# A row softmax on one core: tiles of twelve rows in four buffers, each divided and stored before the next tile's maximum

## Chip, cores and metric

The kernel runs on one core of a Trainium2 chip. The metric is the device time in microseconds, lower is better. DVE is VectorE, ACT is ScalarE, POOL is GpSimd and SP is SyncE; SBUF is the on-chip memory, in 128 partitions. A semaphore is a counter by which one engine, or a transfer, tells another that it is done.

## The reference

```python
batch, seq, dim = 32, 512, 1024          # x: float32, temperature 0.5

def reference(x, temperature):
    scaled = x / temperature
    shifted = scaled - np.max(scaled, axis=-1, keepdims=True)
    exp_x = np.exp(shifted)
    return (exp_x / np.sum(exp_x, axis=-1, keepdims=True)).astype(np.float32)
```

There are 16384 rows of 1024 numbers: 67.1 MB are read and 67.1 MB written.

## The kernel before

A tile gives each of the 128 SBUF partitions eight consecutive rows, so one partition's share is a piece of 32 KiB, contiguous in memory. Loads are issued from SP, stores from ACT. Every load after the first six has to wait for the store that frees its buffer, and six buffers take 192 KiB of each partition. The arithmetic goes in groups of four rows: one maximum on DVE (and a small multiplication that makes the exponentials' bias of it), four exponentials with their sums on ACT, one reciprocal and four multiplications ("divide") on DVE.

```python
TILES = [[8]] * 16
BUFS = 6
GROUP = 4
# ... pools, and `groups`: (tile, first row, rows, the part to store after it)

    def load():
        i = len(tiles)
        if i < len(TILES):
            xt = data.tile([P, sum(TILES[i]), d], f32, name="xt")
            nc.sync.dma_start(out=xt, in_=dram(xf, i))
            tiles.append(xt)
# ... maximum(g), exponential(g), divide(g): as described
    def store(g):
        i, _, _, part = groups[g]
        if part:
            a, k = part
            nc.scalar.dma_start(out=dram(of, i)[:, a : a + k, :], in_=tiles[i][:, a : a + k, :])
            if a + k == sum(TILES[i]):
                load()

    with tc.manual_schedule():
        for _ in range(BUFS):
            load()
        for g in range(len(groups) + 1):
            if g < len(groups):
                maximum(g)
                exponential(g)
            if g > 0:
                divide(g - 1)
                store(g - 1)
```

The order is a software pipeline: group g-1 is divided after the maximum of group g, so that ACT has time for its exponentials. At a tile's end this makes the finished tile wait for the load, and then for the maximum, of the next tile.

Of the kernel before, what the change touches and what calls it, by code (L numbers as in the profile page):

```python
# [1 line left out]

# [4 lines left out]



TILES = [[8]] * 16  # L10
BUFS = 6

GROUP = 4


@with_exitstack
def kernel(
    ctx: ExitStack,
    tc: tile.TileContext,
    x: bass.AP,  # L20
    temperature: bass.AP,
    out: bass.AP,
):
    nc = tc.nc
    f32 = mybir.dt.float32
    scale = 1.0 / float(temperature)
    extreme = mybir.AluOpType.max if scale > 0 else mybir.AluOpType.min

    P = 128
    xf = x.flatten_outer_dims()  # L30
    of = out.flatten_outer_dims()
    n, d = xf.shape
    assert sum(sum(ks) for ks in TILES) * P == n

    data = ctx.enter_context(tc.tile_pool(name="data", bufs=BUFS))
    stats = ctx.enter_context(tc.tile_pool(name="stats", bufs=4))


    groups, first, r = [], [], 0
    for i, ks in enumerate(TILES):  # L40
        first.append(r)
        r += sum(ks)
        a = 0
        for k in ks:
            for b in range(0, k, GROUP):
                m = min(GROUP, k - b)
                groups.append((i, a + b, m, (a, k) if b + m == k else None))
            a += k

    def dram(t, i):  # L50
        k = sum(TILES[i])
        block = t[P * first[i] : P * (first[i] + k), :]
        return block.rearrange("(p k) d -> p k d", p=P, k=k)

    tiles, small = [], []
# [8 lines that stand above are left out]
    def maximum(g):  # L64
        i, a, k, _ = groups[g]
        top, bias, sums, recip = (
            stats.tile([P, k], f32, name=name) for name in ("top", "bias", "sums", "recip")
        )
        small.append((bias, sums, recip))
        nc.vector.tensor_reduce(  # L70
            out=top, in_=tiles[i][:, a : a + k, :], axis=mybir.AxisListType.X, op=extreme
        )
        nc.vector.tensor_scalar_mul(bias, in0=top, scalar1=-scale)  # L73

    def exponential(g):
        i, a, k, _ = groups[g]
        bias, sums, _ = small[g]
        for b in range(k):
            nc.scalar.activation(  # L79
                tiles[i][:, a + b, :],  # L80
                tiles[i][:, a + b, :],
                mybir.ActivationFunctionType.Exp,
                bias=bias[:, b : b + 1],
                scale=scale,
                accum_out=sums[:, b : b + 1],
            )

    def divide(g):
        i, a, k, _ = groups[g]
        _, sums, recip = small[g]  # L90
        nc.vector.reciprocal(recip, sums)  # L91
        for b in range(k):
            nc.vector.tensor_scalar_mul(  # L93
                tiles[i][:, a + b, :], in0=tiles[i][:, a + b, :], scalar1=recip[:, b : b + 1]
# [13 lines that stand above are left out]
        for _ in range(BUFS):  # L108
            load()
        for g in range(len(groups) + 1):  # L110
            if g < len(groups):
                maximum(g)
                exponential(g)
            if g > 0:
                divide(g - 1)
                store(g - 1)


# [1 line left out]
_INS = ['x', 'temperature']  # L120
_OUTS = [((32, 512, 1024), 'float32')]

_NUMBERS = {'temperature': 0.5}


# [26 lines left out]
```

## Time and profile before

| | before |
|---|---|
| time, median of 3 | 317.9 us (317.88 to 318.01) |
| span of the profiled execution | 316.0 us |
| DVE busy, ACT busy | 235.5 us (75%), 149.6 us (47%) |
| moved | 134.25 MB, 425 GB/s over the span |

From the page of the kernel before: the span, the DMA rows of the span cut in 40 slices (a digit is the busy share of the 16 DMA engines in tenths, 9 is 90% or more; below it is what they moved), and two groups of instructions (line, engine, operation, count, then total busy us and mean ns, then the idle time before them and its releaser).

```profile
span 316.0 us, 620 instructions
...
DMA  8999999999999999999999999999999999999996
GB/s 332 411 452 423 373 460 415 452 425 431 436 427 440 427 444 423 444 419 448 415 452 411 452 408 456 423 444 427 436 431 432 440 423 444 419 444 419 452 411 274
...
L70 DVE TENSOR_REDUCE top<-xt 128x4 f32<-128x4096 f32 x32 | 141.3, 4416 | 62.6 <-DMA xt<-in_x_dram 62.6
...
L91 DVE RECIPROCAL recip<-sums 128x4 f32<-128x4 f32 x32 | 5.5, 171 | 2.1 <-ACT xt L79 2.1
```

The DMA engines are busy in every slice but the first and the last; no compute engine is. The next lines are the view by windows: a stretch of the span in us, its length, busy time of DVE, ACT and POOL, the clock, the DMA share, and GB/s.

```profile
core 0: us, DVE busy (x) ACT busy (x) POOL busy (x), PEclk, DMA share, GB/s
2.00:34.00 32.00, 20.69 (x17) 14.63 (x24) 0.00 (x0) 1.00 0.99 422
34.00:60.00 26.00, 25.72 (x25) 14.95 (x27) 0.00 (x0) 1.00 0.99 416
60.00:120.00 60.00, 51.26 (x50) 32.29 (x57) 0.00 (x0) 1.00 1.01 436
120.00:180.00 60.00, 46.15 (x46) 29.79 (x53) 0.00 (x0) 1.00 1.00 432
180.00:240.00 60.00, 44.57 (x43) 29.19 (x51) 0.00 (x0) 1.00 1.00 434
308.00:312.00 4.00, 0.00 (x0) 0.00 (x0) 0.00 (x0) 1.00 1.04 451
312.00:316.00 4.00, 0.00 (x0) 0.00 (x0) 0.00 (x0) 1.00 0.21 90
```

The rate is 416 to 422 GB/s from 2 to 60 us and 432 to 436 from 60 to 240 us; the last transfers are over about 2 us before the end. The two DVE groups on the page show that DVE has time to spare: ahead of its maxima (L70) it is idle for 62.6 us, ended by loads, and ahead of its reciprocals (L91), where it would wait for ACT, for 2.1 us.

The stores, by the view of their source line (durations in ns of the issuing instruction, then the start of the first and of the last issue in us): the first store is issued at 32.7 us.

```profile
L101 ACTq DMA_DIRECT2D out_dram<-xt x16: 338/338/374, 32.7 to 302.4; - x16
```

### The profile page before, as it was taken

Reading aid. Unit: us, or ns where it says so; the run is one execution under the profiler, and the core shown is the slowest. Engines: PE = TensorE matmul, PEld = TensorE weight load, DVE = VectorE, ACT = ScalarE, POOL = GpSimd, SP = SyncE. Lnnn points to the kernel's source line nnn. Section 1 sums busy time; section 2 is a strip of 40 time slices with the busy share of each in tenths; the row PEclk is TensorE's granted clock in tenths of the full one; section 3 lists DMA queues with packets and bytes.
Section 4 is the critical chain, followed back from the end, with each engine's and each line's share of the span. In section 5 each row is a group of like instructions: output and inputs, shape, how many; then the busy total and the mean of one; then the engine's idle time right before and its main releaser. Section 6 shows DMA issues by size and latency. Waiting matters only on the chain.

```text
span 316.0 us, 620 instructions
## 1 busy us (share of the span) xinstructions
DVE 235.5 (75%) x224; ACT 149.6 (47%) x257; POOL 0.2 (0%) x4
## 2 busy tenths in 40 slices
DVE  0399999999689494994949859497693976949720
ACT  0176666666526255361554605546064560645500
POOL 0000000000000000000000000000000000000000
DMA  8999999999999999999999999999999999999996
GB/s 332 411 452 423 373 460 415 452 425 431 436 427 440 427 444 423 444 419 448 415 452 411 452 408 456 423 444 427 436 431 432 440 423 444 419 444 419 452 411 274
DMA packets 4612, 134.25 MB, mean 425 GB/s; under 512 B 512, under 2 KB 512, under 8 KB 512
## 3 DMA queue, kind: packets, MB, share of 16 engines
q1 hardware_dynamic: 2304, 67.11, 49.7%
q10 hardware_dynamic: 2304, 67.11, 49.2%
q14 instruction: 4, 0.03, 0.0%
HBM read 67.11 MB, written 67.11 MB: 425 GB/s over the span
## 4 chain that ended last, share of the span: by engine, by line
DVE 49%; DMA 32%; another core or an unknown queue 9%; ACT 5%; issue 1%; DVEq 0%; SPq 0%
DVE top L70 29%; DMA xt<-in_x_dram 20%; DVE xt L93 18%; DMA out_dram<-xt 12%; ACT xt L79 5%; DVE recip L91 1%; DVE bias L73 1%; DVEq L147 0%; SPq L61 0%
## 5 line engine op out<-in xcount | busy, mean ns | idle before, releaser
L79 ACT ACTIVATE xt<-xt,bias 128x1024 f32<-128x1024 f32 x128 | 145.4, 1137 | 136.8 <-DVE recip L91 119.4
L70 DVE TENSOR_REDUCE top<-xt 128x4 f32<-128x4096 f32 x32 | 141.3, 4416 | 62.6 <-DMA xt<-in_x_dram 62.6
L93 DVE TENSOR_SCALAR xt<-xt,recip 128x1024 f32<-128x1024 f32 x128 | 87.7, 749 | 1.1
L79 ACT ACTIVATION_READ_ACCUMULATOR xt<-xt,bias 128x1 f32 x128 | 23.9, 187 | 0.0
L79 ACT ACT_TABLE_LOAD x1 | 1.3, 1283 | 13.0 <-DMA xt<-in_x_dram 13.0
L91 DVE RECIPROCAL recip<-sums 128x4 f32<-128x4 f32 x32 | 5.5, 171 | 2.1 <-ACT xt L79 2.1
L73 DVE TENSOR_SCALAR bias<-top 128x4 f32<-128x4 f32 x32 | 5.4, 170 | 1.1
L133 POOL MEMSET const-bfloat16-1.0<- 128x1 bf16 x1 | 0.1, 101 | 0.0
L133 POOL MEMSET const-uint8-127<- 128x1 uint8 x1 | 0.1, 101 | 0.0
L133 POOL MEMSET const-float32-0.0<- 128x1 f32 x1 | 0.1, 98 | 0.2 <-issue 0.2
L133 POOL MEMSET const-float32-1.0<- 128x1 f32 x1 | 0.1, 98 | 0.0
## 6 DMA issues: line engine op xcount, KB each, us to landing
xt<-in_x_dram SPq DMA_DIRECT2D x16, 4096.0 KB, 50.2
out_dram<-xt ACTq DMA_DIRECT2D x16, 4096.0 KB, 38.6
```

The source lines that it names most:

```text
L70: nc.vector.tensor_reduce(out=top, in_=tiles[i][:, a : a + k, :], axis=mybir.AxisListType.X, op=extreme)
L73: nc.vector.tensor_scalar_mul(bias, in0=top, scalar1=-scale)
L79: nc.scalar.activation(tiles[i][:, a + b, :], tiles[i][:, a + b, :], mybir.ActivationFunctionType.Exp, bias=bias[:, b : b + 1], scale=scal ...
L91: nc.vector.reciprocal(recip, sums)
L93: nc.vector.tensor_scalar_mul(tiles[i][:, a + b, :], in0=tiles[i][:, a + b, :], scalar1=recip[:, b : b + 1])
L133: nc = _bacc.Bacc("TRN2", target_bir_lowering=False, num_devices=1)
```

## The change

The intent: fewer and larger transfers (22 instead of 32, pieces of 48 KiB instead of 32) in the same 192 KiB, and stores that go out earlier, since a tile's last group is divided before the next tile's maximum.

```diff
@@ -7,8 +7,8 @@
 
 
 
-TILES = [[8]] * 16
-BUFS = 6
+TILES = [[12]] * 10 + [[8]]
+BUFS = 4
 
 GROUP = 4
 
@@ -108,10 +108,14 @@
         for _ in range(BUFS):
             load()
         for g in range(len(groups) + 1):
+            same = 0 < g < len(groups) and groups[g][0] == groups[g - 1][0]
+            if g > 0 and not same:
+                divide(g - 1)
+                store(g - 1)
             if g < len(groups):
                 maximum(g)
                 exponential(g)
-            if g > 0:
+            if same:
                 divide(g - 1)
                 store(g - 1)
```

On DVE the order of instructions changes at tile ends only; the counts and shapes do not.

## The prediction

> **What bounds the kernel now.** The DMA engines. The page shows a DMA share of 9 tenths or more in every slice but the first and last, and 425 GB/s over the 316.0 us span; the busiest compute engine, DVE, has 75%. By stage (busy time per window): 422 GB/s from 2 to 34 us (loads only), 416 to 60 us, then 436, 432, 434 and 430 up to 290 us. The Trainium skill ("DMA: Bandwidth & Descriptors", Where 436 GB/s comes from) puts the fabric's ceiling at 435 GB/s; this trace agrees, its steady state stands at about 433. 134.2 MB at 433 GB/s take 310 us. The other 6 us are the first 2 us (164 GB/s, about 1.2 us lost), the weak stretch up to 60 us (about 2 us) and the last 4 us (90 GB/s, about 3.2 us, mostly the last store's completion). The chain of waits shows much DVE only because it runs back through work that transfers hide: DVE still waits 62.6 us for loads.
>
> **What the change does.** Bytes, compute instructions and their shapes stay (32 maxima of 4.42 us, 128 divisions of 0.75 us, 128 exponentials).
> - A tile's last four rows are divided before the next tile's maximum. Now DVE often waits 4.5 to 5 us for the next load, and then 4.4 us of maximum: stores go out about 9.5 us earlier. In exchange DVE waits at each tile's end for the exponential: four rows take 4.65 us, a division group (2.9 us) covers part, so about 1.8 us a tile. A tile of twelve then costs DVE about 3 x (4.42 + 0.17 + 0.2 + 2.74) + 1.8 = 24.4 us; its load and store cost the DMA 12.58 MB / 433 = 29 us. DMA stays the limit, with 5 us to spare.
> - 22 transfers instead of 32, pieces of 48 KiB instead of 32. Packet time is 98.9% of 16 engines' span over 4096 large packets, 1.22 us each, against 1.20 at 435 GB/s: at most 1.5 us in total can be won from larger pieces.
> - The same 192 KiB per partition. The first tile lands after about 17.5 us instead of 13, the first store goes out near 42 us instead of 32.7. The four first loads last 58 us, so nothing runs dry; loads only, at 422 instead of 433 GB/s, cost 0.3 us more.
> - Tail: now the last store is issued at 302.4 and lands in 12.8 us, almost alone. In a schedule worked out by hand from these durations, the new last store (eight rows) is issued some 10 us before the one ahead of it has drained, so the tail stays full: worth 0 to 1 us.
>
> **On the critical path.** Almost nothing of the 9.5 us per tile: two queues with a backlog keep the engines full whichever gets work earlier. The sum is about 1 us won.
>
> **Prediction.** 316.9 us, range 314.4 to 319.6. Faster by over 2%: 3%; within 2%: 94%; slower by over 2%: 3%.
>
> **What would show it.** Right: DMA share 9 tenths in all inner slices, 428 to 435 GB/s steady; DVE busy unchanged at 235 us; its waits for ACT rise from 2.1 to about 20 us; large packets 2816 instead of 4096; last store landing in about 20 us.
>
> **What would make it wrong.** A piece of 48 KiB that the engines move at another rate (memory pitch, unequal packets): the steady GB/s would show it. Four buffers running dry: a slice of 7 or 8 tenths in the DMA row once stores begin. A last load that comes late: the last slices would show half a DMA.

## The result, and the profile after

| | before | after |
|---|---|---|
| time, median of 6 | 317.97 us (317.88 to 318.09) | 323.01 us (322.37 to 324.42) |
| span profiled | 316.0 us | 322.3 us |
| DVE busy | 235.5 us | 237.0 us |
| GB/s over the span | 425 | 417 |

The ratio is 1.0162, with a 95% interval of 1.0141 to 1.0183. Ratios are the mean time of one kernel's runs over that of the other's of the same rounds, so not quite the ratio of the medians quoted. This is 1.6% slower and clear of the noise, and outside the range predicted. The kernel's own times now also scatter by 2 us, where the kernel before scatters by 0.2. The profiled execution, with 324.42 us, is the slowest of the six.

The same parts of the page, for the changed kernel:

```profile
span 322.3 us, 600 instructions
...
DMA  8999999999999999999999999999999999999993
GB/s 329 445 409 464 403 390 433 378 403 380 415 433 427 403 464 409 464 415 451 427 421 451 409 433 428 439 439 427 451 427 403 440 443 409 441 447 427 429 405 150
...
L70 DVE TENSOR_REDUCE top<-xt 128x4 f32<-128x4096 f32 x32 | 141.3, 4415 | 42.5 <-DMA xt<-in_x_dram 42.5
...
L91 DVE RECIPROCAL recip<-sums 128x4 f32<-128x4 f32 x32 | 5.6, 176 | 23.3 <-ACT xt L79 23.3
```

The windows of the changed kernel:

```profile
core 0: us, DVE busy (x) ACT busy (x) POOL busy (x), PEclk, DMA share, GB/s
2.00:34.00 32.00, 15.33 (x10) 10.45 (x17) 0.00 (x0) 1.00 0.99 427
34.00:60.00 26.00, 23.70 (x25) 14.19 (x25) 0.00 (x0) 1.00 1.00 403
60.00:120.00 60.00, 52.28 (x52) 31.93 (x56) 0.00 (x0) 1.00 0.99 411
120.00:180.00 60.00, 46.44 (x45) 27.62 (x48) 0.00 (x0) 1.00 1.01 435
180.00:240.00 60.00, 46.02 (x43) 29.10 (x51) 0.00 (x0) 1.00 1.01 433
312.00:316.00 4.00, 0.00 (x0) 0.00 (x0) 0.00 (x0) 1.00 1.03 442
316.00:320.00 4.00, 0.00 (x0) 0.00 (x0) 0.00 (x0) 1.00 0.27 115
```

This is where the time went. The DMA share is as full as before (0.99 to 1.01), but between 34 and 120 us the engines move only 403 and 411 GB/s, where they moved 416 and 436. Full engines, fewer bytes: each packet takes longer. From 120 us on the rates are equal (435 and 433 against 432 and 434). Then the end drags: from 316 to 320 us the mean DMA share is 0.27, so a few engines are still at work and the others have nothing left.

The DVE groups of the page show what the new order does: DVE is idle for 23.3 us ahead of its reciprocals, waiting for ACT, and for 42.5 us instead of 62.6 ahead of its maxima.

The stores:

```profile
L101 ACTq DMA_DIRECT2D out_dram<-xt x11: 338/338/377, 42.9 to 305.1; - x11
```

### What the packet records add

The trace has a record of every DMA packet (queue, start, duration, size, but not which of the 16 engines), and of the 16 increments of each transfer's semaphore. The Trainium skill ("DMA: Bandwidth & Descriptors", Why a DMA increments its semaphore by 16 and not by 1) says that each engine adds one when its own share has landed; this trace agrees in that every transfer here has 16 increments, and their times differ. From these records four numbers were worked out, used from here on:

- *Normal packet time*: the median is 1213 ns for 32 KiB and 1815 ns for 48 KiB, in every run. That is 27.0 and 27.1 GB/s for one engine and 432 to 433 for sixteen; the same page (Where 436 GB/s comes from) has 435 for the fabric, so the two agree within 1%.
- *Slow time*: what packets took beyond the median of their size, summed and divided by 16. Before: 1.68 us an engine. After: 5.65 us.
- *Spread at the end*: the time between the first and the last of the 16 increments of the last store. Before: 1.8 us (313.4 to 315.2). After: 5.4 us (316.0 to 321.4).
- *Distance*: load packets started minus store packets started, divided by 16. It says how many packets one engine's loads are ahead of its stores. A tile is 128 pieces, so 8 packets for each engine, whatever their length.

The span grew by 6.3 us. The first engine to finish ends 2.6 us later than before, and the spread adds 3.6 us; together 6.2.

The slow packets after the start lie for the most part between 42 and 107 us (4.3 of 5.0 us an engine; about 1 us of it comes as the first store begins, where the kernel before loses 0.8 us too). They are of both queues and come in bursts, most of them of 5 to 11 packets within some 2 us. The distance tells what is peculiar there: it is 23.9 on average from 55 to 75 us, so the loads are three whole tiles ahead and both queues work on the same row of their tiles. Before, it stands at 27.2 (26.8 to 27.6 in stretches of 10 us). When the first four loads of the changed kernel are done and the next load must wait for the first store, the distance falls to about 21, and the slow packets become fewer and soon rare.

The distance keeps its value because loads and stores take turns. One engine of the kernel before, put together from the records by matching each packet's end with the next one's start (start in us; L and S are load and store packets of this engine, numbered from 0; every one took 1213 ns):

```
44.62 S3   45.83 L31  47.04 S4   48.26 S5   49.47 L32  50.68 S6
51.89 L33  53.09 S7   54.30 L34  55.52 L35  56.73 S8   57.94 L36
```

The turns are strict but for one place at each end of a transfer, where a queue misses one turn (S4 and S5 where a load tile ends, L34 and L35 where a store tile ends). The Trainium skill (the same page, Queues, rings and completion order) has the engine go round the queues at packet granularity; the trace agrees, with single pieces of 32 KiB as the unit. With strict turns, the distance is fixed once, by how many loads have gone when the first store starts, until a queue runs dry; the table below shows it, where the distances of 55 to 75 us and of 100 to 240 us agree on tiles of eight rows.

### The profile page after: what moved, and what is told of

It reads as the page before. It is cut to its first block, busy times and chain, and to the rows that moved or that the text cites. A ratio compares the mean times of both kernels' runs of the same rounds, so it can differ in the third digit from the quotient of the medians.

```text
span 322.3 us, 600 instructions
## 1 busy us (share of the span) xinstructions
DVE 237.0 (74%) x224; ACT 148.6 (46%) x257; POOL 0.2 (0%) x4
## 4 chain that ended last, share of the span: by engine, by line
DMA 51%; another core or an unknown queue 18%; DVE 16%; ACT 9%; issue 0%; DVEq 0%; SPq 0%; ACTq 0%
DMA xt<-in_x_dram 39%; DMA out_dram<-xt 12%; DVE top L70 10%; ACT xt L79 9%; DVE xt L93 6%; DVE bias L73 0%; DVE recip L91 0%; DVEq L151 0%; SPq L61 0%; ACTq L79 0%
## 5 line engine op out<-in xcount | busy, mean ns | idle before, releaser
L70 DVE TENSOR_REDUCE top<-xt 128x4 f32<-128x4096 f32 x32 | 141.3, 4415 | 42.5 <-DMA xt<-in_x_dram 42.5
L79 ACT ACTIVATION_READ_ACCUMULATOR xt<-xt,bias 128x1 f32 x128 | 23.9, 187 | 0.0
L91 DVE RECIPROCAL recip<-sums 128x4 f32<-128x4 f32 x32 | 5.6, 176 | 23.3 <-ACT xt L79 23.3
L79 ACT ACT_TABLE_LOAD x1 | 1.3, 1283 | 18.4 <-DMA xt<-in_x_dram 18.4
## 6 DMA issues: line engine op xcount, KB each, us to landing
out_dram<-xt ACTq DMA_DIRECT2D x1, 4096.0 KB, 16.3
```

The lines of the kernel that those rows point to most:

```text
L70: nc.vector.tensor_reduce(out=top, in_=tiles[i][:, a : a + k, :], axis=mybir.AxisListType.X, op=extreme)
L79: nc.scalar.activation(tiles[i][:, a + b, :], tiles[i][:, a + b, :], mybir.ActivationFunctionType.Exp, bias=bias[:, b : b + 1], scale=scal ...
L91: nc.vector.reciprocal(recip, sums)
```

## The experiments

Theories at the start: A, that packets of 48 KiB are slowed where loads and stores mix; B, that the new order costs the time through DVE's waits. After the first four runs a third took their place. P: the moment of the first store sets the distance between the two streams, and at some distances packets are slow, in any kernel of this kind. Fifteen kernels ran, each timed in 3 rounds against the kernel before.

| run | distance 55-75 us | distance 100-240 us | slow time an engine | spread at the end | median | ratio, 95% interval |
|---|---|---|---|---|---|---|
| (before) | 27.2 | 27.2 | 1.68 us | 1.8 us | 318.0 us | |
| (after) | 23.9 | 20.8 | 5.65 us | 5.4 us | 323.0 us | 1.0162 (1.0141-1.0183) |
| e1 size only | 25.4 | 21.3 | 2.24 us | 0.7 us | 319.8 us | 1.0049 (1.0012-1.0085) |
| e2 order only | 25.4 | 25.4 | 5.94 us | 2.4 us | 323.9 us | 1.0179 (1.0153-1.0205) |
| e3 half pieces | (35.4) | (35.6) | 1.67 us | 2.0 us | 318.8 us | 1.0018 (0.9996-1.0040) |
| e4 blocks of 8 and 4 | (35.6) | (35.4) | 1.74 us | 2.0 us | 318.5 us | 1.0011 (0.9985-1.0038) |
| e12 order only, first store +2 | 26.3 | 26.3 | 1.63 us | 2.5 us | 318.0 us | 1.0003 (0.9988-1.0018) |
| e5 order only, first store +4 | 27.8 | 27.9 | 1.63 us | 2.1 us | 318.2 us | 0.9997 (0.9982-1.0012) |
| e11 order only, first store +10 | 33.8 | 33.8 | 4.54 us | 5.2 us | 322.0 us | 1.0133 (1.0115-1.0150) |
| e6 before, first store +5 | 32.6 | 32.6 | 1.85 us | 2.0 us | 318.4 us | 1.0011 (0.9988-1.0034) |
| e10 before, first store +6 | 33.8 | 33.8 | 5.48 us | 3.6 us | 322.0 us | 1.0129 (1.0114-1.0144) |
| e14 before, first store +7 | 34.3 | 34.2 | 1.57 us | 1.8 us | 317.9 us | 1.0005 (0.9988-1.0022) |
| e15 after, first store +3 | 25.4 | 19.8 | 2.87 us | 6.7 us | 324.1 us | 1.0202 (1.0144-1.0260) |
| e7 after, first store +7 | 27.6 | 21.7 | 2.16 us | 2.4 us | 318.3 us | 1.0008 (0.9988-1.0029) |
| e8 after, loads shifted | 22.6 | 22.4 | 2.42 us | 2.3 us | 319.5 us | 1.0050 (1.0002-1.0097) |
| e9 order only, loads shifted | 25.4 | 25.4 | 5.75 us | 2.4 us | 324.4 us | 1.0208 (1.0191-1.0225) |
| e13 order only, loads issued later | 25.4 | 25.4 | 5.30 us | 0.2 us | 327.5 us | 1.0303 (1.0287-1.0318) |

Slow time, distance and spread come from each run's one profile, which need not be a typical run: that of e1 was the fastest of its four (318.53 us, median 319.8), that of e8 the second fastest. "First store +2" means held back by two dummy instructions. The runs were made on several chips, each beside the kernel before on the same chip, and the ratio compares these two. In e3 and e4 a tile is two transfers and more packets, so their distances (in brackets) do not compare with the others.

### The parts of the change, and the pieces

e1 is the change without its order, e2 without its size:

```diff
 e1 (from before)                      e2 (from before)
-TILES = [[8]] * 16                    the new loop, with
-BUFS = 6                               TILES = [[8]] * 16
+TILES = [[12]] * 10 + [[8]]            BUFS = 6
+BUFS = 4
```

> The size of the change alone (twelve rows, four buffers), with the old order: a tile is divided after the maximum of the next. Theory A (48 KiB packets, mixed loads and stores, are slowed on some DMA engines just after stores begin, and the slowest engine ends late): the loss is here already, 321 to 324.5 us, packets of 49152 bytes longer than 1.87 us by the dozen between 40 and 100 us. Theory B (the new order, which makes DVE wait at each tile's end, costs the time): this runs at 316.5 to 318.5 us. The old order with four buffers holds one tile back for the next load, so a further loss through dry queues is possible: then DMA slices below 9 tenths.

> The order of the change alone, with tiles of eight rows in six buffers. Theory A: no loss, 316.5 to 318.5 us, hardly any packet of 32768 bytes over 1.27 us after 40 us. Theory B: 321 us or more, with DVE waiting for ACT at each of 16 tile ends.

Measured: 319.8 us (318.53 to 321.0), between the ranges of both theories, and 323.94 us. Theory A falls with e2: pieces of 32 KiB are as slow, with 263 of 4096 packets over 50 ns above the median after the first 5 us. Theory B got its number, but the two parts do not add: 0.5% and 1.8% alone, 1.6% together. In e2 the slow packets come at the place in each tile where one store ends and the next begins, 1 to 3 packets after a load tile began; they are load packets in the main. Not all of e1's loss is slow packets: from 288 to 290 us of its profile the DMA share is 0.17, as both queues run dry for a moment.

e3 halves the transfers of the changed kernel, e4 makes each tile of a block of eight rows and one of four:

```diff
 e3
-nc.sync.dma_start(out=xt, in_=dram(xf, i))
+h = sum(TILES[i]) // 2
+for a in (0, h):
+    nc.sync.dma_start(out=xt[:, a : a + h, :], in_=dram(xf, i)[:, a : a + h, :])
 (the store likewise)
 e4: dram(t, i) returns blocks of at most 8 rows, each contiguous; one transfer each
```

> The changed kernel, each load and store cut in two transfers of six rows: the pieces are 24 KiB, but a partition's pieces still lie 48 KiB apart in memory, and tiles, buffers and order are those of the change. Theory A1 (the length of a packet is what hurts): 316.5 to 318.5 us. Theory A2 (the distance of 48 KiB in memory hurts): 321 us or more, with slow packets of 24576 bytes between 40 and 100 us.

> The changed kernel, each tile of twelve rows made of a block of eight rows a partition (32 KiB pieces, 32 KiB apart) and one of four (16 KiB, 16 KiB apart), two transfers each way; tiles, buffers and order are those of the change. Theories A1 and A2 both expect 316.5 to 318.5 us and few slow packets. A rival A3 (the number and size of tiles: fewer, larger units of work start the stores late, at 43 us, and the trouble belongs to that start): 321 us or more.

Measured: 318.78 and 318.49 us, without the slow stretch. By themselves they look like a verdict for the length of a packet (A1). Beside e2, which is slow with 32 KiB, they are not: both also moved the first store (issued at 31.7 and 33.0 us instead of 42.9) and the number of packets to a tile. With the new order and a size of twelve both still there, the waits of DVE for ACT are there too (22.7 and 34.8 us in their waits) and the time is not lost. That speaks against B.

### Moving the first store

The sharpest test is to move the first store and to change nothing else in the code. Dummy exponentials on ACT, which read the finished tile and write a spare buffer, hold it back. One takes 1.14 us, but the store moves by less where ACT would have waited anyway: by 1.1 us with two of them (e12), 3.2 with four (e5), 7.3 with seven in the changed kernel (e7):

```diff
+DELAY = 4
+idle = ctx.enter_context(tc.tile_pool(name="idle", bufs=1)).tile([P, d], f32, name="idle")
     def store(g):
         if part:
             a, k = part
+            for _ in range(DELAY if i == 0 else 0):
+                nc.scalar.activation(idle, tiles[0][:, a + k - 1, :], ...Exp)
             nc.scalar.dma_start(...)
```

> The order alone on tiles of eight rows (323.9 us), with the first store of all held back by four dummy exponentials on ScalarE, about 2.8 us; every later instruction is the same. Theory P (phase): loads and stores take turns on each DMA engine, so their distance in rows, set once by the moment of the first store, stays; the trace of the order alone shows a load 25.2 rows ahead of the store (three tiles of eight, plus 1.2) and slow load packets at each tile's end, that of before 27.5 rows and none. Held back to about 27.5 rows, this should run at 317.5 to 319.5 us. Theory B (the new order itself costs the time, by the waits of DVE for ACT): 323 us or more, as the delay can only add.

> The kernel before (318.0 us), with its first store held back by five dummy exponentials, about 5.6 us, so that the loads should be some 32 rows ahead: a whole number of tiles of eight, as in the changed kernel between 42 and 78 us. Theory P: 321 us or more, with slow packets of both queues in the steady part. Theory B, or any theory of the order or of the size: at most the delay matters, and it is hidden, so 317.5 to 319.5 us.

> The changed kernel (323.0 us), with its first store held back by seven dummy exponentials, about 6.2 us or 3.4 rows of 48 KiB: instead of exactly 24 rows (three piece counts of eight) the loads are some 27.4 ahead, until the loads of the first four tiles are done and the distance falls to about 21. Theory P: 318 to 320 us, few slow packets between 45 and 80 us. Theory B, or theory A (pieces of 48 KiB are slow when mixed): 322.5 us or more.

Measured: e5 318.15 us. A delay added to one store took the order-only kernel from 323.9 to 318.2 us, with every wait of the new order in place. Theory B is out. e7 318.32 us: the changed kernel, given seven useless instructions, is as fast as the kernel before. Its first store, and its windows from 34 to 120 us, where the changed kernel had 403 and 411 GB/s:

```profile
L107 ACTq DMA_DIRECT2D out_dram<-xt x11: 337/338/376, 50.2 to 297.7; - x11
```

```profile
34.00:60.00 26.00, 20.83 (x22) 20.78 (x30) 0.00 (x0) 1.00 0.99 412
60.00:120.00 60.00, 53.41 (x55) 32.61 (x58) 0.00 (x0) 1.00 1.00 433
```

e6 was a miss: 318.36 us, not slow. So a distance near a whole number of tiles is not bad as such on pieces of 32 KiB. The order-only kernel had stood at three tiles and 1.4 packets, e6 at four tiles and 0.6. The next runs looked there:

> The kernel before with its first store held back by six dummy exponentials instead of five, so that the loads are 33.5 rows ahead: four whole tiles and 1.5 rows, where the slow order-only kernel has three whole tiles and 1.4, and the run with five dummies 4 tiles and 0.6. Theory P with a period of one tile: 320 us or more. If only the absolute distance of 24 to 25.5 rows is bad, 317.5 to 319 us.

> The order alone with its first store held back by ten dummy exponentials, loads some 33.4 rows ahead. As for the run before it: 320 us or more if the bad distance repeats with every tile, 317.5 to 319.5 us if not.

> The order alone with its first store held back by two dummy exponentials, loads some 26 rows ahead instead of 25.4 (slow) or 27.9 (not slow). It tells how wide the bad distance is: theory P allows anything between, 318 to 324 us, and expects the time to go with the count of slow load packets; theory B expects 323 us or more.

> The kernel before with seven dummy exponentials ahead of its first store, loads some 34.4 rows ahead. The order-only kernel was slow at 25.4 rows and fast at 26.2 to 26.8; with five dummies (32.6 rows) this kernel was fast, with six (33.7) slow. If the bad stretch is one row wide and repeats every eight rows, seven dummies (2.4 rows past a whole tile) give 317.8 to 319 us again; if everything from 33 rows up is bad, 321.5 us or more.

Measured: 322.03, 322.02, 317.97 and 317.94 us. The kernel before, with five, six and seven dummies, takes 318.4, 322.0 and 317.9 us. Its size and its order are untouched. And e12, with its first store issued only 1.1 us later than e2, loses nothing where e2 loses 1.8%. The lines of their stores and their windows from 120 to 240 us, e2 first:

```profile
L101 ACTq DMA_DIRECT2D out_dram<-xt x16: 338/338/376, 30.0 to 307.2; - x16
120.00:180.00 60.00, 47.59 (x44) 30.40 (x54) 0.00 (x0) 1.00 1.00 427
180.00:240.00 60.00, 45.32 (x44) 28.35 (x51) 0.00 (x0) 1.00 1.01 422
```

```profile
L107 ACTq DMA_DIRECT2D out_dram<-xt x16: 338/338/376, 31.1 to 301.1; - x16
120.00:180.00 60.00, 50.34 (x49) 33.67 (x59) 0.00 (x0) 1.00 1.01 435
180.00:240.00 60.00, 45.00 (x44) 28.86 (x52) 0.00 (x0) 1.00 1.00 431
```

The profiles of e6, e10 and e14, first the line of their stores (look at the start of the first one), then the windows 60 to 240 us.

Five dummies (e6):

```profile
L107 ACTq DMA_DIRECT2D out_dram<-xt x16: 338/338/374, 38.7 to 296.4; - x16
```

```profile
60.00:120.00 60.00, 53.46 (x53) 36.42 (x64) 0.00 (x0) 1.00 1.01 435
120.00:180.00 60.00, 45.08 (x43) 27.82 (x48) 0.00 (x0) 1.00 1.00 430
180.00:240.00 60.00, 45.36 (x43) 27.82 (x48) 0.00 (x0) 1.00 1.01 434
```

Six dummies (e10):

```profile
L107 ACTq DMA_DIRECT2D out_dram<-xt x16: 338/338/377, 40.0 to 299.6; - x16
```

```profile
60.00:120.00 60.00, 54.56 (x56) 37.10 (x64) 0.00 (x0) 1.00 1.01 425
120.00:180.00 60.00, 44.19 (x42) 27.82 (x48) 0.00 (x0) 1.00 1.00 424
180.00:240.00 60.00, 44.21 (x43) 27.82 (x48) 0.00 (x0) 1.00 1.00 426
```

Seven dummies (e14):

```profile
L107 ACTq DMA_DIRECT2D out_dram<-xt x16: 338/338/374, 41.0 to 293.9; - x16
```

```profile
60.00:120.00 60.00, 57.21 (x57) 37.10 (x64) 0.00 (x0) 1.00 1.01 437
120.00:180.00 60.00, 45.76 (x43) 27.83 (x48) 0.00 (x0) 1.00 1.00 432
180.00:240.00 60.00, 45.53 (x45) 27.82 (x48) 0.00 (x0) 1.00 1.00 433
```

The first store moves by 1.3 and 1.0 us, and the steady rate, at a DMA share of 1.00 to 1.01 in all three, goes from 430-435 down to 424-426 and up again to 432-437 GB/s. In both orders the distances of three tiles and 1.4 packets (e2) and four tiles and 1.8 (e10, e11) are slow, and 0.6 (e6), 2.2 (e14), 2.3 (e12), 3.2 (before) and 3.9 (e5) are not. So on pieces of 32 KiB the bad stretch was met after three tiles and after four; taking the two together, it covers 1.4 to 1.8 packets past a whole tile and does not reach 0.6 or 2.2. Between 3.9 packets and the next whole tile nothing was tried.

One more for the changed kernel:

> The changed kernel with three dummy exponentials instead of seven ahead of its first store: its loads should be about 25 rows ahead of the first store instead of 24.2 (323.0 us) or 28 (318.3 us). The size-only kernel had 25.9 rows there and took 319.8 us. Theory P expects it between, 318.5 to 322 us, with fewer slow packets between 45 and 80 us than the changed kernel; a theory that only a long delay helps expects 322.5 us or more.

Measured: 324.09 us, from 322.25 to 326.99, above the range given. It was a miss, and an instructive one: slow time is only 2.87 us an engine, yet the spread at the end is 6.7 us. The increments of its last store show 15 engines done between 315.1 and 316.8 us and one at 321.8. The increments of earlier transfers show when the last of the 16 fell behind the second last: by 4.0 us in a transfer that landed at 80.5 us, with the distance at 25.4 until about 70 us, and by 6.0 in one that landed at 107.9, when the distance had fallen to about 20. It never caught up. So part of this loss came at another distance than 25.4. The size-only kernel, e1, passed the same distance and lost little. With pieces of 48 KiB, then, a distance of 23.9 is bad (the changed kernel against e7); that 25.4 is bad too is suggested by e15 and not shown, as e1 and e15 differ at it.

### What it is not

Two runs read the input some way further on, so that the addresses of loads and stores in flight stand otherwise to each other. Their outputs are wrong, which doesn't matter for the times.

```diff
+SHIFT = 42        # e8, from after: 168 KiB.  e9, from order only: 28 rows, 112 KiB
-            nc.sync.dma_start(out=xt, in_=dram(xf, i))
+            at = dram(xf, i) if i == len(TILES) - 1 else shifted(i)
+            nc.sync.dma_start(out=xt, in_=at)
```

> The changed kernel, wrong on purpose: every load but the last reads 42 rows (168 KiB, three and a half pieces) further on in the input, so that the addresses of loads in flight stand otherwise to those of the stores, while queues, SBUF partitions and times are as in the changed kernel. Theory P1 (it is the addresses in HBM that load and store have in common that make packets slow): 318 to 320 us. Theory P2 (it is the common row, that is the common SBUF partition or place in the ring, whatever the address): 322 to 324.5 us as the changed kernel.

> The order alone on tiles of eight rows (323.9 us; loads 25.4 rows ahead all through), wrong on purpose: every load but the last reads 28 rows (112 KiB, three and a half pieces) further on in the input; queues, times and SBUF places stay. Theory P1 (slow packets come of the addresses that load and store have in HBM at the same time): 317.5 to 320 us, with the loads still some 25 rows ahead. Theory P2 (they come of the distance in rows, partitions or ring places, whatever the address): 322.5 to 325 us.

Measured: e8 319.52 us (318.4 to 321.94), e9 324.39 us. They seem to contradict each other. But in e8 the distance did not stay: it was 22.6 and not 23.9, so its better time can come of the distance or of the addresses, and e8 settles nothing. e9 kept its 25.4 and its slow packets, at the same places. So for this shift, at least, the memory address is not what counts.

e13 asks whether it is the issue of the next load, which in e2 falls just where the slow packets are, as SP issues it when the store lands:

```diff
             xt = data.tile([P, sum(TILES[i]), d], f32, name="xt")
+            if i >= BUFS:
+                nc.gpsimd.memset(xt[:, 0:HOLD, :], 0.0)      # HOLD = 6
             nc.sync.dma_start(out=xt, in_=dram(xf, i))
```

> The order alone on tiles of eight rows (323.9 us, loads 25.4 rows ahead), with each load of a freed buffer issued some microseconds after the store has landed, as GpSimd first fills three quarters of the buffer with zeros. The queue of loads holds more than a tile at that time, so the packets should not move and the distance should stay near 25.4 rows. If the slow packets come of issuing a load while another load tile starts: 318 to 320 us. If they come of the two streams' packets whatever is being issued: 322.5 to 325 us. If the distance changes, or DVE slows beside GpSimd, it says nothing.

Measured: 327.53 us. The time says nothing, as DVE slowed beside GpSimd (267.2 us busy instead of 238.2) and the last store was late. By its own expectation the run then says nothing; what follows is a reading of its packets made afterwards. Each fill took 5.2 us, the loads were issued that much later, and the slow packets stayed where they were, 5.30 us an engine at a distance of 25.4: in e13 as in e2 most are load packets 1 to 3 after a load tile began, as a store begins. So the issue of the load is not the cause. The run bears on one more rival as well: a dummy on ACT shifts the later work of ACT and DVE too, not the first store alone. e13 shifts that work more, at the same distance, and the slow packets stay.

## Why the prediction was wrong

- *What bounds the kernel, and its parts*: right. DMA was the limit and stayed it. The packets came to 2816, as predicted; DVE stayed at 237.0 us (235 predicted); its waits for ACT rose to 23.3 us (about 20 predicted); the first store went out at 42.9 us (near 42); the first tile landed at 18.4 us (about 17.5).
- *The step that failed*: "two queues with a backlog keep the engines full whichever gets work earlier", and from it "Almost nothing of the 9.5 us per tile" and "428 to 435 GB/s steady" in all. The engines were full, as it said (a DMA share of 0.99 to 1.00 from 34 to 120 us). But full is not a fixed rate: at some distances between the streams a packet takes longer. The rate was 403 and 411 GB/s from 34 to 120 us, at a distance of 23.9 until 78 us, and packets took 5.65 us an engine beyond the normal instead of 1.68. The moment of the first store, which the prediction worked out correctly and put at a cost of 0.3 us, is what set the distance. e7 shows it for the changed kernel, and e5, e10 and e12 for others.
- *Larger pieces, up to 1.5 us won*: not seen. The median packet runs at 27.0 (32 KiB) and 27.1 GB/s (48 KiB), so there was nothing to win there.
- *The tail, 0 to 1 us won*: a loss came in its place. The last store was issued at 305.1 us (the hand schedule had it wait some 10 us behind the one ahead) and landed in 16.3 us (about 20 predicted), but the 16 engines ended 5.4 us apart instead of 1.8. The prediction reckoned with one backlog for all 16 together.
- *What would make it wrong*: "A piece of 48 KiB that the engines move at another rate" was near to the symptom, and pointed to a false cause: e2, with 32 KiB, is just as slow, and e7, with 48 KiB, is not.
- *Chances*: within 2% was given 94%, and the ratio of 1.0162 does lie there; but a gain of about 1 us was forecast and a loss of 5 us came, so that this says nothing for its reasoning.

The new order by itself cost nothing once the first store was moved (e12, e5), and nor did the whole change (e7). The size moved the first store and, with four buffers, changed the distance again after 78 us; which distances are bad on pieces of 48 KiB was not mapped. What stays open: why a distance of 1.4 to 1.8 packets past a whole tile (of 32 KiB pieces), or of three whole tiles (of 48 KiB), makes packets slow. It is not the issue of a load (e13), and not the memory address at the one shift tried (e9). Whether it is the SBUF partitions that both streams then share, or the turns that both queues miss within a packet or two of each other, no run separates; in e6, at 0.6 packets past a whole tile, where the missed turns of 32 KiB pieces should lie closest together, next to nothing is slow (1.85 us an engine).

No run beat the kernel before: the best ones come to its 318 us and no lower.

## What to carry to other kernels

Where loads and stores fill the DMA engines together, a full DMA row did not mean a fixed rate here: read GB/s beside the share, stage by stage, and the spread of the last transfer's 16 increments for engines that ended late. Moving the first store by 1.0 to 1.3 us cost or gave back 1.2 to 1.8% in three pairs of runs (e6 and e10, e10 and e14, e2 and e12), by the distance at which the two streams then ran, so before a change of tile size or order is judged, or kept, time it with the first store moved by one or two packets. Setting a good distance on purpose won back a loss here; it gained nothing over the kernel before.

## What the Trainium skill lacked or had wrong

- No page has it that two queues taking turns run slower at some distances. "DMA: Bandwidth & Descriptors" gives one rate by size and the fabric's ceiling; here the same 4 MiB transfers ran at 424-426 or 430-437 GB/s by a delay of 1 us in the first store (e10 against e6 and e14).
- "DMA: Bandwidth & Descriptors" (Queues, rings and completion order) lacks the missed turn: at the end of each transfer its queue skips one turn and the other queue gets two packets of 1213 ns in a row.
- The same page lacks what a first store does to the loads that it joins: in every trace load packets are slow about when it begins, 0.8 us an engine before, 1.0 after, and 0.5 to 1.2 in the other runs.
- The rule to coalesce into the largest single transfer ("SBUF — State Buffer", The DMA setup-cost knee) brought nothing from 4 to 6 MiB with queues that kept the DMA row full: the median packet ran at 27.0 and 27.1 GB/s, and the halved transfers of e3, at a distance that is not bad, took 318.8 us, within 0.3% of the kernel before.
- "SBUF — State Buffer" (Who interferes with whom) says that DVE and GpSimd can block each other at a shared port pair, for the whole of an instruction. e13 agrees: beside each of its ten fills on GpSimd, of 5.2 us, DVE started a bias multiplication and a reciprocal, and both lasted until the fill ended (2.4 to 4.3 us instead of 0.17). The maxima that ran beside the fills kept their 4.41 us. No multiplication of 1024 numbers ran beside a fill.
